# Second feed-forward products by Strassen's seven-product scheme, in a kernel of eight transformer stages

## The chip, the cores and the metric

The kernel runs on one core of one Trainium2 chip. The metric is the device time of one execution in microseconds (us). The kernel before takes 2401.51 us (median of 3 runs, 2397.78 to 2402.21).

## The reference, cut to what matters

Two blocks of two layers each run over 512 tokens of width 1024 in float32. The second block has a feed-forward part in each of its layers, and the change touches these two alone:

```python
def squared_relu_mlp(u, w1, w2):
    return jnp.square(jax.nn.relu(u @ w1)) @ w2
...
        u = squared_relu_mlp(rms_norm(h, g_ff_pre[l]), w_ff1[l], w_ff2[l])
        h = h + rms_norm(u, g_ff_post[l])
```

`w1` is 1024 x 4096 and `w2` is 4096 x 1024. Their two products have the same number of multiplications.

## The kernel before

The program is a row of eight stages (`STAGES`); `ff0` and `ff1` are the fifth and the last. All weights lie in one array `ws`, in the order in which they are used: tiles of 128 x 2048 numbers (1 MB) that hold 1024 x 256 or 512 x 512 weights.

**Three passes for float32.** Each operand is split into a rounded high part and the rest. ScalarE (ACT) copies it to the rounded type, VectorE (DVE) subtracts that copy from the original. `mm3` then issues three matmuls for each product: high x high, low x high, high x low. For weights the split makes `whi` and `wlo` (L257, L258, two halves of 128 x 1024 each); for the activations in the feed-forward, `yh` and `yl` (L355, L356). `weights` splits one tile ahead of the one in use and has the transfer of the tile after that under way: `raw` has three buffers, `whi` and `wlo` two of 128 x 2048 each.

**The feed-forward stage (`ff`).** It goes over the 4096 features in four groups of 1024. In a group, eight units (`unit`) of 24 matmuls make 128 features each for all 512 tokens, in a PSUM bank `pj` (three of them). ACT takes the relu (L1222), DVE squares it (L1223), and the result `r` is split. The second product then takes four PSUM banks, one for each 128 tokens, for each half of the 1024 output columns: 2 x 4 x 24 = 192 matmuls for a group, all of 128 x 512. DVE adds each bank into `acc` (L1247). GpSimd (POOL) does nothing in these groups. At the last group, `second_half` interleaves the norm and the transposes of the next stage (`boundary`, `norm_T`).

**The start of the stage.** Before the stage opens, `begin` has done the first 256 tokens of the first four units; when it opens, only 24 short matmuls of each of the four are left.

**What sets the order.** A scheduler turns the program into one fixed queue for each engine. An instruction waits at the head of its queue for the others by semaphores, and everything behind it waits too. SyncE (SP) issues the weight transfers in order, each when its buffer has been read.

Of the kernel before, what the change touches and what calls it, by code (L numbers as in the profile page):

```python
# [41 lines left out]
def stream_order(stages):  # L42
# [14 lines left out]
    for st in stages:  # L57
# [24 lines left out]
        elif st in ("x0", "x1"):  # L82
            for h in range(4):
                span("xq" + st[1], 256 * h)
            outw("xo" + st[1])
        elif st in ("ff0", "ff1"):
            for q in range(4):
                for j in range(4):
                    span("ff1_" + st[2], q * 1024 + j * 256)
                outw("ff2_" + st[2], q * 1024)  # L90
# [15 lines left out]
def host_arrays(inputs, stages):  # L106
# [15 lines left out]
    for n, (key, kind, sel) in enumerate(order):  # L122
        a = w[key]
        if kind == "cols":
            b = a[:, list(sel)].reshape(8, P, 256)
        else:
# [63 lines left out]

class Prog:
    def __init__(self, ctx, tc, a, out, stages):
# [4 lines left out]
        self.wt = {}  # L197

# [40 lines left out]
    def _dma(self, n):  # L239
        if n >= len(self.order) or ("r", n) in self.wt:  # L240
            return
        r = []
        for half in range(2):
            t = self.wp.tile([P, 1024], F32, tag="raw", name="raw", bufs=3)
            self.nc.sync.dma_start(out=t, in_=self.a["ws"][n, :, half * 1024:(half + 1) * 1024])
            r.append(t)
        self.wt["r", n] = r

    def _split(self, n):
        if n >= len(self.order) or n in self.wt:  # L250
            return
        self._dma(n)
        hi = self.wp.tile([P, 2048], F32R, tag="whi", name="whi", bufs=2)
        lo = self.wp.tile([P, 2048], F32R, tag="wlo", name="wlo", bufs=2)
        for half, t in enumerate(self.wt.pop(("r", n))):
            s = slice(half * 1024, (half + 1) * 1024)
            self.nc.scalar.activation(out=hi[:, s], in_=t, func=AF.Copy)  # L257
            self.nc.vector.tensor_sub(out=lo[:, s], in0=t, in1=hi[:, s].bitcast(F32))  # L258
        self.wt[n] = (hi, lo)
        self.wt["r", n] = None  # L260

    def weights(self, key):
# [6 lines left out]
        self._split(n)  # L269
        self._split(n + 1)  # L270
        self._dma(n + 2)
        hi, lo = self.wt.pop(n)
        c = 256 if self.order[n][1] == "cols" else 512
        return n, hi.rearrange("p (k c) -> p k c", c=c), lo.rearrange("p (k c) -> p k c", c=c)

    def mm3(self, ps, pairs, first=True, last=True, between=None):

        n = len(pairs)
        for k, ((ah, al), (bh, bl)) in enumerate(pairs):
            if between and k == n // 2:  # L280
# [930 lines left out]
    def ff(self, l, stage):  # L1211
        nc = self.nc
        with self.pool(f"ff{l}") as p:
            acc = [p.tile([P, D], F32, tag=f"acc{t}", name=f"acc{t}") for t in range(NT)]
            for q in range(4):
                y = []
                for j in range(4):
                    w = self.weights(f"ff1_{l}")
                    for m in range(2):
                        ps = self.unit(w, m)  # L1220
                        r = p.tile([P, S], F32, tag="r", name="r", bufs=2)
                        nc.scalar.activation(out=r, in_=ps, func=AF.Relu)  # L1222
                        nc.vector.scalar_tensor_tensor(out=r, in0=ps, scalar=0.0, in1=r, op0=ALU.max, op1=ALU.mult)  # L1223
                        y.append(self.split_y(r))
                if q == 3:
                    self.begin_out(stage, p)
                for c in range(2):
                    cs = slice(c * 512, (c + 1) * 512)
                    if q == 3 and c == 1:
                        def done(t, ps):  # L1230
                            nc.vector.tensor_tensor(out=acc[t][:, cs], in0=acc[t][:, cs], in1=ps, op=ALU.add)
                            self.boundary(t, (acc[t][:, :512], acc[t][:, 512:]), self.h[:, t, :], stage, p)

                        self.second_half(f"ff2_{l}", y, done)
                        continue
                    pa = [self.ps(tag) for tag in ("sc", "sc", "pv", "pj")]
                    for kh in range(2):
                        _, hi, lo = self.weights(f"ff2_{l}")
                        for t in range(NT):
                            tok = slice(t * P, (t + 1) * P)  # L1240
                            self.mm3(pa[t], [((y[kh * 4 + k][0][:, tok], y[kh * 4 + k][1][:, tok]), (hi[:, k, :], lo[:, k, :]))
                                             for k in range(4)], first=kh == 0, last=kh == 1)
                    for t in range(NT):
                        if q == 0:
                            self.copy(acc[t][:, cs], pa[t])
                        else:
# [219 lines left out]
```

## Time and profile before

| | us |
|---|---|
| median of 3 runs | 2401.51 |
| profiled execution | 2402.01 |
| its span, first to last instruction | 2400.2 |
| TensorE (PE) busy | 2349.0, 98% |
| DVE busy | 1278.6, 53% |
| ACT busy | 930.4, 39% |
| POOL busy | 269.9, 11% |
| stage `ff0`, about | 1346 to 1700 |
| stage `ff1`, about | 2050 to 2400 |

TensorE is busy almost without a break. Matmuls are pipelined: one is listed with the time from its start to its end, but the next starts earlier. What a matmul costs is therefore read from the distance between starts. What another engine's work costs is read from who waits for it.

### The profile page before, as it was taken

The numbers are of one execution on the slowest core, as the hardware profiler recorded it, in microseconds if no ns is written. First come the engines' busy times: TensorE is split into PE (matmuls) and PEld (weight loads), VectorE is DVE, ScalarE is ACT, GpSimd is POOL, SyncE is SP. The second block draws the span as 40 slices with busy tenths as digits, with TensorE's granted clock in tenths as the row PEclk, the third lists the DMA queues.
The fourth block names the chain that finished last, engine by engine and source line by source line (L and its number), as shares of the span: only waits on it lengthen the run. The fifth ranks groups of instructions, "written<-read, shape, count | busy, mean of one in ns | idle before, by whom it ended". The sixth has DMA issues, their size and how long they took to land.

```text
span 2400.2 us, 33303 instructions
## 1 busy us (share of the span) xinstructions
PE 2349.0 (98%) x13008; PEld 1947.0 (81%) x13008; DVE 1278.6 (53%) x2370; ACT 930.4 (39%) x1843; POOL 269.9 (11%) x315
## 2 busy tenths in 40 slices
PE   7999999999999999999999999999999999999998
PEld 7879788787888878877988888888866988888887
DVE  5364655546665546664644633435786645533434
ACT  3333333333444444453533422323465534432322
POOL 3010111101211112000200100000211201000000
PEclk9999999999999999999999999999999999999999
DMA  5433333334232322223331332322322422332322
GB/s 167 129 102 119 98 116 91 108 93 129 99 100 86 98 91 93 76 70 114 123 123 71 106 101 92 104 90 88 99 84 97 141 89 80 106 105 89 103 90 79
DMA packets 94172, 242.39 MB, mean 101 GB/s; under 512 B 26700, under 2 KB 30828, under 8 KB 94016
## 3 DMA queue, kind: packets, MB, share of 16 engines
q1 hardware_dynamic: 93216, 238.34, 30.4%
q8 instruction: 102, 1.67, 0.3%
q0 software_dynamic: 800, 1.94, 0.3%
q14 instruction: 54, 0.44, 0.1%
HBM read 215.98 MB, written 4.33 MB: 92 GB/s over the span
## 4 chain that ended last, share of the span: by engine, by line
PE 63%; DVE 4%; issue 2%; ACT 2%; POOL 2%; DMA 1%; SPq 0%; POOLq 0%; DVEq 0%; ACTq 0%
PE pj L282 14%; PE pj L284 13%; PE pj L283 13%; PE sc L282 3%; PE sc L283 3%; PE sc L284 3%; PE pv L282 2%; PE pv L284 2%; PE pv L283 2%; PE sc L1325 1%; DVE h L431 1%; PE sc L775 1%; DVE wlo L258 1%; PE pv L797 1%; PE pt L401 1%
## 5 line engine op out<-in xcount | busy, mean ns | idle before, releaser
L258 DVE TENSOR_TENSOR wlo<-raw,whi 128x1024 fp32r<-128x1024 f32 x372 | 473.4, 1294 | 498.0 <-ACT whi L257 498.0
L257 ACT ACTIVATE whi<-raw 128x1024 fp32r<-128x1024 f32 x372 | 382.7, 1055 | 538.7 <-PE pj L284 216.7
L282 PE MATMUL pj<-uh,whi 128*128 128x512 f32 (+1 forms) x1424 | 561.4, 394 | 0.8 <-ACT ho L1101 0.8
L284 PE MATMUL pj<-uh,wlo 128*128 128x512 f32 (+1 forms) x1424 | 551.8, 388 | 1.6 <-DVE wlo L258 1.6
L283 PE MATMUL pj<-ul,whi 128*128 128x512 f32 (+1 forms) x1424 | 550.6, 387 | 0.0
L282 PEld LDWEIGHTS pj<-uh,whi 128*128 128x128 f32 x1424 | 267.6, 188 | 73.7 <-issue 17.1
L284 PEld LDWEIGHTS pj<-uh,wlo 128*128 128x128 f32 x1424 | 267.6, 188 | 60.0 <-issue 3.8
L283 PEld LDWEIGHTS pj<-ul,whi 128*128 128x128 f32 x1424 | 267.9, 188 | 52.1 <-issue 2.4
L513 POOL TENSOR_TENSOR ro<-rt 128x512 f32<-128x512 f32 x74 | 112.8, 1535 | 657.6 <-DVE rt L511 587.9
L282 PE MATMUL pj<-whi,uh 128*128 128x256 f32 x608 | 174.9, 288 | 0.0
L283 PE MATMUL pj<-wlo,uh 128*128 128x256 f32 x608 | 172.5, 284 | 0.0
L284 PE MATMUL pj<-whi,ul 128*128 128x256 f32 x608 | 171.9, 283 | 0.0
L282 PE MATMUL pj<-whi,yh 128*128 128x512 f32 x416 | 164.1, 395 | 1.4 <-ACT yh L355 1.1
L283 PE MATMUL pj<-wlo,yh 128*128 128x512 f32 x416 | 162.6, 391 | 0.9 <-DVE wlo L258 0.9
L284 PE MATMUL pj<-whi,yl 128*128 128x512 f32 x416 | 162.6, 391 | 0.0
L376 POOL TENSOR_SCALAR rs<-ss 128x1 f32<-128x1 f32 x32 | 23.1, 722 | 1089.0 <-ACT bq L422 1088.8
L282 PE MATMUL sc<-whi,yh 128*128 128x512 f32 x320 | 126.8, 396 | 0.1
L283 PE MATMUL sc<-wlo,yh 128*128 128x512 f32 x320 | 125.8, 393 | 0.0
L284 PE MATMUL sc<-whi,yl 128*128 128x512 f32 x320 | 125.2, 393 | 0.0
L282 PEld LDWEIGHTS pj<-whi,uh 128*128 128x128 f32 x608 | 116.4, 191 | 4.6 <-ACT at L231 2.3
L283 PEld LDWEIGHTS pj<-wlo,uh 128*128 128x128 f32 x608 | 116.5, 192 | 0.5 <-issue 0.2
L284 PEld LDWEIGHTS pj<-whi,ul 128*128 128x128 f32 x608 | 116.4, 192 | 0.2 <-issue 0.2
(364 smaller groups left out, 3833.4 us busy)
## 6 DMA issues: line engine op xcount, KB each, us to landing
raw<-in_ws_dram SPq DMA_DIRECT2D x372, 512.0 KB, 4.0
qk<-ro SPq DMA_DIRECT2D x256, 64.0 KB, 2.0
gpre<-in_gains_dram SPq DMA_DIRECT2D x8, 512.0 KB, 5.6
gpost<-in_gains_dram SPq DMA_DIRECT2D x8, 512.0 KB, 5.2
xt<-in_x_dram SPq DMA_DIRECT2D x4, 512.0 KB, 8.1
dv<-v SPq DMA_DIRECT2D x4, 512.0 KB, 4.1
v<-dv SPq DMA_DIRECT2D x16, 128.0 KB, 4.7
h<-in_x_dram SPq DMA_DIRECT2D x4, 512.0 KB, 5.6
```

The costliest lines, as they stand in the source:

```text
L257: self.nc.scalar.activation(out=hi[:, s], in_=t, func=AF.Copy)
L258: self.nc.vector.tensor_sub(out=lo[:, s], in0=t, in1=hi[:, s].bitcast(F32))
L282: self.nc.tensor.matmul(ps, lhsT=ah, rhs=bh, start=first and k == 0, stop=False)
L283: self.nc.tensor.matmul(ps, lhsT=ah, rhs=bl, start=False, stop=False)
L284: self.nc.tensor.matmul(ps, lhsT=al, rhs=bh, start=False, stop=last and k == n - 1)
L376: nc.gpsimd.tensor_scalar(out=r[:, 0:1], in0=ss[:, 0:1], scalar1=ss[:, 1:2], scalar2=EPS, op0=ALU.add, op1=ALU.add)
L401: nc.tensor.transpose(pt[:, k * P:(k + 1) * P], b[:, (4 * g + k) * P:(4 * g + k + 1) * P], self.ident)
L431: nc.vector.scalar_tensor_tensor(out=h, in0=b, scalar=r, in1=h, op0=ALU.mult, op1=ALU.add)
L513: nc.gpsimd.tensor_tensor(out=o, in0=t[0], in1=t[1], op=op)
L775: nc.tensor.matmul(ps[:, :n], lhsT=q[hs, 0, i * P:n], rhs=q[hs, 1, :n], start=True, stop=True)
L797: nc.tensor.matmul(o[:, i * P:(i + 1) * P], lhsT=at[:, j * P:(j + 1) * P], rhs=v[h // 2][:, j, (h % 2) * P:(h % 2 + 1) * P], start=j == 0, ...
L1325: nc.tensor.matmul(ps[e][:, hp * 256 + lo:(hp + 1) * 256], lhsT=q[hs, hp, i * P:(i + 1) * P], rhs=kd[hs, g, (i - 1) * P + lo:(i + 1) * P], ...
```

## The change

**The scheme.** In seven of eight blocks of 512 features, the second product is no longer done as one sum. The left matrix (512 tokens x 512 features) is cut in halves both ways, into A11, A12 (first 256 tokens) and A21, A22; the weights (512 features x 1024 columns) into B11, B12, B21, B22 of 256 x 512. In place of eight products of quarters there are seven: A11 B11, A12 B21, S2 T2, S1 T1, S3 T3, S4 B22 and A22 T4, where each S is a sum or difference of A quarters and each T one of B quarters. A product is 12 matmuls of 128 x 512, so a block has 84 where the old way needs 96. The eighth block of each stage is done the old way, so that the norm can be interleaved with it.

**Sums on GpSimd.** `quad_sums` makes T3, T1, T2, T4 in place in the buffers that hold the weights (tag `quad`, five buffers), four instructions of 128 x 1024 for a block. `operands` makes S1 to S4 for each of the two pairs of feature chunks, j = 0, 1 of a block: four instructions of 128 x 256 each, two in tile `s12`, two in tile `s34`. Before, GpSimd had none of these.

**Splits.** Weights are split by halves of 128 x 1024 (`whi` and `wlo` now have four such buffers): 11 for a block of 512 features, four of `w1` and seven of the B's and T's, where the old way needs four and four. The left operands are split from `r`, `s12` and `s34`: 128 x 512, 256, 512 and 512 columns for each j, where two of 128 x 512 were needed.

**Banks.** A12 B21, S1 T1 and S4 B22 gather in six PSUM banks over all seven blocks (`sums`) and are added to `acc` once. The other four products go through two `pj` banks (`chain`), added to `acc` after each; the same two banks serve the units of the next block, since the third holds a sum.

The descriptor memory of the GpSimd queue shrinks too (`dynamic_dma_scratch_size=4096`). The bytes of weights stay the same.

```diff
+            for q in range(8):
+                for j in range(2):
+                    span("ff1_" + st[2], q * 512 + j * 256)
+                if q < 7:
+                    for m in range(2):
+                        out.append(("ff2_" + st[2], "quad", (q * 512 + m * P, m)))
...
+QUADS = ("B11", "B21", "T2", "T1", "T3", "B22", "T4")
...
+            for m, name in enumerate(("B11", "B12", "B21", "B22")):
+                q[name] = self.qp.tile([P, 1024], F32, tag="quad", name="quad", bufs=5)
+                self.nc.sync.dma_start(out=q[name], in_=self.a["ws"][n + m // 2, :, (m % 2) * 1024:(m % 2 + 1) * 1024])
...
+    def _fill(self, m):
+
+        while len(self.ready) < m and self.done < len(self.halves):
+            n, name = self.halves[self.done]
+            self._dma(n)
+            if n not in self.wt:
+                return
+            t = self.wt[n].get(name)
+            hi = self.wp.tile([P, 1024], F32R, tag="whi", name="whi", bufs=4)
+            lo = self.wp.tile([P, 1024], F32R, tag="wlo", name="wlo", bufs=4)
+            self.parts((hi, lo), t)
...
+    def quad_sums(self, n, first):
+
+        q = self.wt[n]
+        sub = lambda name, x, y: (self.nc.gpsimd.tensor_tensor(out=q[name], in0=q[x], in1=q[y], op=ALU.subtract))
+        if first:
+            q["T3"] = self.qp.tile([P, 1024], F32, tag="quad", name="quad", bufs=5)
+            sub("T3", "B22", "B12")
+            q["T1"] = q["B12"]
+            sub("T1", "B12", "B11")
+        else:
+            q["T2"], q["T4"] = q["B11"], q["B21"]
+            sub("T2", "B22", "T1")
+            sub("T4", "B21", "T2")
...
+            def operands(ya, yb):
+
+                h = slice(0, 256), slice(256, S)
+                s12, s34 = (p.tile([P, S], F32, tag=n, name=n, bufs=2) for n in ("s12", "s34"))
+                for out, x, z, op in ((s12[:, h[0]], ya[:, h[1]], yb[:, h[1]], ALU.add), (s12[:, h[1]], s12[:, h[0]], ya[:, h[0]], ALU.subtract),
+                                      (s34[:, h[0]], ya[:, h[0]], ya[:, h[1]], ALU.subtract), (s34[:, h[1]], yb[:, h[0]], s12[:, h[1]], ALU.subtract)):
+                    nc.gpsimd.tensor_tensor(out=out, in0=x, in1=z, op=op)
+                res = {}
+                for names, t in ((("A12", "A22"), yb), (("A11",), ya), (("S1", "S2"), s12), (("S3", "S4"), s34)):
...
+            for q in range(7):
+                ops = []
+                n = self.order.index((f"ff2_{l}", "quad", (q * 512, 0)))
+                for j in range(2):
+                    w = self.weights(f"ff1_{l}")
+                    self._dma(n)
+                    if j == 1:
+                        self._fill(2)
+                    self.quad_sums(n, j == 0)
+                    ops.append(operands(*features(w)))
+                self.pos += 2
+                chain = [self.ps("pj") for _ in range(2)]
+                for left, acc_of in (("A11", (0, 0)), ("A12", None), ("S2", (0, 1)), ("S1", None), ("S3", (1, 1)), ("S4", None), ("A22", (1, 0))):
+                    (hi, lo), = self._take(1)
...
+                        ps = chain[t] if acc_of else sums[left][t]
+                        self.mm3(ps, [([z[:, tok] for z in ops[j][left]], (hi[:, j, :], lo[:, j, :])) for j in range(2)],
+                                 first=left == "A11" if acc_of else q == 0, skip_group_check=True)
+                        if acc_of:
+                            add(2 * acc_of[0] + t, acc_of[1], ps, q == 0)
```

**Where the instructions stand.** Three places, first as it was and then as it is. In the names, the number behind a tile tells buffers apart.

POOL, start of `ff0`. Before, the last norm of the boundary is followed at once by that of the next boundary:

```order
L390 TENSOR_TENSOR bu_12019<-h_5610,gpre_11673 128x320
L378 TENSOR_SCALAR rs_12025<-ss1_12021 128x1
L379 TENSOR_TENSOR rs_12025<-rs_12025,mhalf_80 128x1
L376 TENSOR_SCALAR rs_14273<-ss_14268 128x1
L379 TENSOR_TENSOR rs_14273<-rs_14273,mhalf_80 128x1
```

Now the twelve sums of the first block stand between them (the first nine are shown). In order they are: first half of `s34` for j = 0, T3, T1, T2, first half of `s12`, T4, second halves of `s12` and `s34`, then j = 1.

```order
L439 TENSOR_TENSOR rs_12099<-rs_12099,mhalf_80 128x1
L1303 TENSOR_TENSOR s34_12434<-r_12403 128x256
L325 TENSOR_TENSOR quad_12376<-quad_12374,quad_12370 128x1024
L325 TENSOR_TENSOR quad_12370<-quad_12370,quad_12368 128x1024
L325 TENSOR_TENSOR quad_12368<-quad_12374,quad_12370 128x1024
L1303 TENSOR_TENSOR s12_12433<-r_12403,r_12430 128x256
L325 TENSOR_TENSOR quad_12372<-quad_12372,quad_12368 128x1024
L1303 TENSOR_TENSOR s12_12433<-s12_12433,r_12403 128x256
L1303 TENSOR_TENSOR s34_12434<-r_12430,s12_12433 128x256
L1303 TENSOR_TENSOR s34_12520<-r_12489 128x256
```

So `s12` of j = 0 is complete only after all four T's.

PE, a middle block, where the second product begins. Before, the first matmuls take features that were split long ago:

```order
L284 MATMUL pj_12970<-uh_11675,wlo_12855 128x512
L282 MATMUL sc_13002<-whi_12928,yh_12744 128x512
L283 MATMUL sc_13002<-wlo_12929,yh_12744 128x512
L284 MATMUL sc_13002<-whi_12928,yl_12745 128x512
L282 MATMUL sc_13002<-whi_12928,yh_12776 128x512
```

Now 16 matmuls that need only j = 0 come first (`yh_13077`, `yh_13073`, `yh_13081`); the last of them, and the first of j = 1 (`yh_13161`, then `yh_13165`), are:

```order
L342 MATMUL sc_12602<-whi_13197,yh_13081 128x512
L342 MATMUL pj_13178<-whi_13089,yh_13077 128x512
L343 MATMUL pj_13178<-wlo_13090,yh_13077 128x512
L344 MATMUL pj_13178<-whi_13089,yl_13078 128x512
L342 MATMUL pt_12565<-whi_13093,yh_13161 128x512
L342 MATMUL pj_13177<-whi_13089,yh_13165 128x512
```

The last unit's output is thus wanted 16 matmuls after that unit ends.

DVE, where the second product of a middle block ends. Before, the four adds follow two splits, and nothing stands between them:

```order
L258 TENSOR_TENSOR wlo_13065<-raw_13012,whi_13064 128x1024
L258 TENSOR_TENSOR wlo_13065<-raw_13014,whi_13064 128x1024
L1247 TENSOR_TENSOR acc0_12182<-acc0_12182,sc_13002 128x512
L1247 TENSOR_TENSOR acc1_12183<-acc1_12183,sc_13003 128x512
L1247 TENSOR_TENSOR acc2_12184<-acc2_12184,pv_13004 128x512
L1247 TENSOR_TENSOR acc3_12185<-acc3_12185,pj_13005 128x512
```

Now (B21's buffer `quad_13004` holds T4, and the `raw` rows are weights of the next block's units):

```order
L416 TENSOR_TENSOR wlo_13248<-quad_13004,whi_13247 128x1024
L416 TENSOR_TENSOR wlo_13270<-raw_13251,whi_13269 128x1024
L1285 TENSOR_TENSOR acc2_12366<-acc2_12366,pj_13177 128x512
L1285 TENSOR_TENSOR acc3_12367<-acc3_12367,pj_13178 128x512
L416 TENSOR_TENSOR wlo_13286<-raw_13253,whi_13285 128x1024
L416 TENSOR_TENSOR wlo_13308<-raw_13289,whi_13307 128x1024
L1285 TENSOR_TENSOR acc2_12366<-acc2_12366,pj_13177 128x512
L1285 TENSOR_TENSOR acc3_12367<-acc3_12367,pj_13178 128x512
```

The last add out of the first `chain` bank (`pj_13177`), which the next block's first unit writes next, stands behind a split of weights for that block's third unit (`wlo_13308`).

## Rows read from the trace of the kernel before

**Rows 1.** The page: busy us (share of the span) and instructions

```profile
PE 2349.0 (98%) x13008; PEld 1947.0 (81%) x13008; DVE 1278.6 (53%) x2370; ACT 930.4 (39%) x1843; POOL 269.9 (11%) x315
```

**Rows 2.** Busy us (instructions) by stretch: PE, PEld, DVE, ACT, POOL; clock, DMA share, GB/s

```profile
1345.00:1700.00 355.00, 351.70 (x1647) 294.43 (x1646) 157.13 (x182) 117.45 (x164) 14.44 (x20) 1.00 0.28 95
2050.00:2380.00 330.00, 328.86 (x1511) 274.64 (x1510) 134.52 (x159) 103.85 (x138) 2.17 (x5) 1.00 0.27 93
```

**Rows 3.** Timeline of PE in `ff1` (start, us, instruction): two starts, 24 matmuls apart

```profile
2139.82 0.39 PE L282 MATMUL pj<-uh,whi 128*128 128x512 f32 x1
...
2145.26 0.39 PE L282 MATMUL pj<-uh,whi 128*128 128x512 f32 x1
```

**Rows 4.** From one unit's end to its split features: timelines of PE, ACT, DVE

```profile
1428.47 0.39 PE L282 MATMUL pj<-uh,whi 128*128 128x512 f32 x1
...
1428.67 0.60 ACT L1222 ACTIVATE r<-pj 128x512 f32<-128x512 f32 x1 [2.95 <-PE pj L284]
...
1429.30 0.69 DVE L1223 SCALAR_TENSOR_TENSOR r<-pj,r 128x512 f32<-128x512 f32 x1 [2.13 <-ACT r L1222]
...
1430.02 0.63 ACT L355 ACTIVATE yh<-r 128x512 fp32r<-128x512 f32 x1 [0.76 <-DVE r L1223]
...
1430.68 0.69 DVE L356 TENSOR_TENSOR yl<-r,yh 128x512 fp32r<-128x512 f32 x1 [0.70 <-ACT yh L355]
```

**Rows 5.** ACT and DVE: a weight half on ACT, two on DVE, an add

```profile
1433.93 1.06 ACT L257 ACTIVATE whi<-raw 128x1024 fp32r<-128x1024 f32 x1 [3.28 <-PE pj L283]
...
1403.05 2.36 DVE L258 TENSOR_TENSOR wlo<-raw,whi 128x1024 fp32r<-128x1024 f32 x2 [3.61 <-ACT whi L257]
...
1483.07 0.69 DVE L1247 TENSOR_TENSOR acc<-acc,sc 128x512 f32<-128x512 f32 x1 [1.39 <-PE sc L284]
```

**Rows 6.** POOL: ns min/median/max of its two kinds of wide instructions

```profile
L513 POOL TENSOR_TENSOR ro<-rt x74: 1275/1305/2287, 38.2 to 1793.0; 128x512 f32<-128x512 f32 x74
...
L390 POOL TENSOR_TENSOR bu<-h,gpre x28: 876/1523/1584, 627.6 to 2049.0; 128x320 f32<-128x320 f32 x28
```

**Rows 7.** Timelines of DVE and POOL where both are busy

```profile
103.84 0.68 DVE L511 TENSOR_TENSOR rt<-pj,sin 128x512 f32<-128x512 f32 x1
104.44 3.43 DVE L258 TENSOR_TENSOR wlo<-raw,whi 128x1024 fp32r<-128x1024 f32 x2
...
102.74 1.31 POOL L513 TENSOR_TENSOR ro<-rt 128x512 f32<-128x512 f32 x1 [45.30 <-DVE rt L511]
104.65 2.13 POOL L513 TENSOR_TENSOR ro<-rt 128x512 f32<-128x512 f32 x1 [0.60 <-DVE rt L511]
```

**Rows 8.** Start of `ff0`: PE's first short matmul and first full one; first relu, square

```profile
1346.20 0.28 PE L282 MATMUL sc<-uh,whi 128*128 128x256 f32 x1
...
1357.72 0.40 PE L282 MATMUL pj<-uh,whi 128*128 128x512 f32 x1
...
1349.28 0.60 ACT L1222 ACTIVATE r<-sc 128x512 f32<-128x512 f32 x1 [3.71 <-PE sc L284]
...
1349.91 0.69 DVE L1223 SCALAR_TENSOR_TENSOR r<-sc,r 128x512 f32<-128x512 f32 x1 [3.56 <-ACT r L1222]
```

**Rows 9.** Transfers: issue to landing of weight halves (KB, median us); SP's issue before `ff0`

```profile
raw<-in_ws_dram SPq DMA_DIRECT2D x372, 512.0 KB, 4.0
...
1339.42 0.42 SPq L368 DMA_DIRECT2D gpost<-in_gains_dram  x1
```

**Rows 10.** A long wait of PE: timeline, then the clock by stretch (columns as Rows 2)

```profile
1128.88 1.17 PE L401 MATMUL pt<-ident,bu 128*128 128x128 f32 x8 [3.99 <-DVE bu L393]
...
1131.13 0.63 PE L282 MATMUL sc<-whi,yh 128*128 128x512 f32 x1
1131.56 0.63 PE L283 MATMUL sc<-wlo,yh 128*128 128x512 f32 x1
...
1130.00:1131.00 1.00, 1.00 (x4) 0.81 (x3) 1.00 (x2) 1.00 (x3) 0.00 (x0) 0.50 0.00 0
1132.00:1133.00 1.00, 1.00 (x4) 0.81 (x3) 1.00 (x2) 0.00 (x0) 0.00 (x0) 0.50 0.97 393
```

**Rows 11.** PE's waits for weight splits (us in total, times, longest)

```profile
PE pj L284 <- DVE wlo L258: 1.6, 1, 1.6
...
PE pj L283 <- DVE wlo L258: 0.9, 1, 0.9
```

More of the change, by code (lines that the diff above doesn't have):

```diff
@@ L86, in stream_order @@
         elif st in ("ff0", "ff1"):
[L87 to L90, printed above, removed]
+            for q in range(8):
[5 more added lines that the diff above has]
+                else:
+                    for c in range(2):
+                        out.append(("ff2_" + st[2], "rows", (q * 512, c * 512)))
         elif st == "sw":
@@ L1213, in ff @@
         with self.pool(f"ff{l}") as p:
+            self.qp = p
             acc = [p.tile([P, D], F32, tag=f"acc{t}", name=f"acc{t}") for t in range(NT)]
-            for q in range(4):
-                y = []
-                for j in range(4):
-                    w = self.weights(f"ff1_{l}")
[L1219 to L1226, printed above, removed]
-                for c in range(2):
[L1228 to L1246, printed above, removed]
-                            nc.vector.tensor_tensor(out=acc[t][:, cs], in0=acc[t][:, cs], in1=pa[t], op=ALU.add)
@@ new lines, in ff, with add, features @@
+            sums = {}
+            def add(t, c, ps, new=False):
+                out = acc[t][:, c * 512:(c + 1) * 512]
+                if new:
+                    self.copy(out, ps, "s")
+                else:
+                    nc.vector.tensor_tensor(out=out, in0=out, in1=ps, op=ALU.add)
+            def features(w):
+                y = []
+                for m in range(2):
+                    ps = self.unit(w, m)
+                    r = p.tile([P, S], F32, tag="r", name="r", bufs=4)
+                    nc.scalar.activation(out=r, in_=ps, func=AF.Relu)
+                    nc.vector.scalar_tensor_tensor(out=r, in0=ps, scalar=0.0, in1=r, op0=ALU.max, op1=ALU.mult)
+                    y.append(r)
+                return y
@@ new lines, in ff @@
+            y = []
+            for j in range(2):
+                y += [self.split_y(z) for z in features(self.weights(f"ff1_{l}"))]
+                if j == 0:
+                    for t in range(2):
+                        add(t, 0, sums["A12"][t])
+                        add(2 + t, 1, sums["S1"][t])
+                        add(t, 1, sums["S1"][t])
+                        add(t, 1, sums["S4"][t])
+            self.qp = None
+            self.begin_out(stage, p)
+            w = [self.weights(f"ff2_{l}")[1:] for _ in range(2)]
@@ new lines, in part, with done @@
+            def part(ps, t, c):
+                tok = slice(t * P, (t + 1) * P)
+                self.mm3(ps, [((y[k][0][:, tok], y[k][1][:, tok]), (w[c][0][:, k, :], w[c][1][:, k, :])) for k in range(4)])
+                add(t, c, ps)
+            def done(t):
+                self.boundary(t, (acc[t][:, :512], acc[t][:, 512:]), self.h[:, t, :], stage, p)
+            for t in range(2 if self.next else NT):
+                for c in range(2):
+                    part(self.ps("pj"), t, c)
+                done(t)
```

91 lines of the change are left out of this document (63 added, 28 removed).

## The prediction

> **What bounds the kernel now.** I read the busy shares first: TensorE (PE) is busy 98% of the span [rows 1], and in the two feed-forward stages more than that, 351.7 of 355 us and 328.9 of 330 us [rows 2]. So these stages are priced by matmuls, as long as PE never waits. A matmul of 128 x 512 costs the distance between starts: 24 of them take 2145.26 - 2139.82 = 5.44 us, 0.2267 us each [rows 3]. VectorE (DVE) works under half of that time there, GpSimd (POOL) 2 to 14 us of it [rows 2]. The question is whether the removed matmuls stay removed, or come back as waits.
>
> **What the change removes.** Twelve matmuls in each of seven blocks in two stages: 168 x 0.2267 = 38.1 us. All of it is on the path, since PE has no slack there.
>
> **What it adds beside PE.** A block of 512 features is now 4 units x 24 + 84 = 180 matmuls, 40.8 us. The work of the others in a block, from rows:
> - DVE: 11 weight halves at 1.14 (two in 2.36 with their overlap [rows 5]), 12.5; squares 4 x 0.6 and adds 8 x 0.6 (0.69 alone [rows 4, 5], some 0.6 in a row), 7.2; left operands 2 x (0.6 + 0.35 + 0.6 + 0.6), 4.3. Together 24 us.
> - POOL: an instruction of 512 columns takes 1.29, one of 320 columns 0.88 [rows 6], so 2.16 ns a column on 0.19 us. That gives 2.4 for 1024 columns and 0.74 for 256, as estimates; the trace has neither. A block's 4 T sums and 8 S sums are 9.6 + 5.9 = 15.5 us.
>
> By shares both fit into 40.8 us. But the two engines do not run side by side. A DVE pair of weight splits alone takes 2.36 us [rows 5]; where a POOL instruction falls into it the pair takes 3.43 and the POOL instruction 2.13 in place of 1.3 [rows 7]. 1.07 more on the one and 0.83 on the other is what comes out if each runs alone and they take turns. A DVE instruction that reads PSUM (L511) beside a POOL instruction keeps its 0.68 [rows 7]. So splits from SBUF (`wlo`, `yl`) exclude POOL's sums; squares and adds, which read PSUM, do not. The Trainium skill ("SBUF — State Buffer", section "Who interferes with whom") speaks against this change in the same way: the shared port pair is an exclusive lock, and a DVE instruction with two SBUF inputs blocks GpSimd for its whole length or is blocked by it. The trace agrees (3.43 against 2.36), and the sum without that lock is the first rival below. The skill also has a price for the sums ("GPSIMD Engine Reference", section "Elementwise — side-by-side cycle accounting"): 4497 ns for 2048 columns of float32, so about 2.25 for 1024, an estimate. By it each T sum would be 0.15 us shorter and the total some 2 us lower.
>
> With that I follow the fixed queues, alternating whenever both want to go. From a unit's end to its square's end takes 1.5 us, to `yh` 2.2, to `yl` 2.9 [rows 4].
>
> **First block of a stage (q = 0).** Only four half units of 2.88 us are left when the stage opens: 11.52 us [rows 8], and then the products begin. POOL's first sum waits for the first square, 4.4 us in [rows 8]; the T's behind it wait too, though their weights are there (the transfers can go at about 1339, where SP issued its last ones before the stage [rows 9], and land in some 4 to 8 us). Complete `s12` for j = 0 needs 0.74 + 3 x 2.4 + 0.74 + 2.4 + 0.74 = 11.8 us of POOL, and between these DVE takes its turns with B11, B21, two left operands and T2: 3 x 1.15 + 0.95 = 4.4 us. So it is there at 4.5 + 11.8 + 4.4 = 20.7, and its `yh` at 21.4. PE has 12 matmuls to do until then, to 14.2: **7.2 us of waiting**. Next, ACT's queue has the relu of the last unit behind the `yh` of `s34`: 21.5 + 0.65 + 0.6, its square 0.7, T1's copy beside it, its `yh` 0.65: 24.4, where PE had two matmuls, to 21.9: **2.5**. Then the two `yl` of that unit, which alternate with T1's split and the sums of j = 1, at 26.8 and 27.9: **1.9**. Sum 11.6 us. PE then has been idle for over 3 us twice. After a wait of 3.99 us the granted clock was 0.50, the lower level, for some 3 us, and matmuls came 0.43 apart in place of 0.23 [rows 10]; seven of them cost 1.5 us. I add that once: 13.1 us a stage, 26 in both. Bounds: 5.3 a stage if nothing excludes anything (POOL's 11.8 us alone still end at 16.3, 2.8 late, and the relu costs 2.5), 16 if the clock falls twice and POOL is 10% slower.
>
> **Begin of the products, blocks 1 to 6.** Count from the products' first matmul. Sixteen matmuls that need only j = 0 cover 3.6 us, and the last unit's `yh` is there at 2.2: no wait. The wait comes at matmul 28, at 6.35 us, which rewrites the first `chain` bank and needs the add out of it. That add stands on DVE behind all four left operands of j = 1, and these need POOL. By turns: square 1.5, first half of `s12` 2.34, `yl` 2.95, second half of `s12` 3.7, `yl` 4.05, `s34` 4.8, `yl` of `s12` 5.45, of `s34` 6.15, add 6.75: 0.5 late with the semaphore. And the square is late itself: POOL can form T2 only after B11's split, and T2 and T4 (31.1 to 35.95 after the previous block's products began) stand ahead of `s12` and `s34` of j = 0. By turns their `yl` end at 40.55, the third unit's square at 41.15, POOL's next sum at 42.0, the splits of T2 and T1 at 44.3, while the products begin at 42.8; the last unit's square follows at 44.3 in place of 43.6, 0.65 late. **1.2 us a block**, 12 blocks, 14 us. Bounds 0 and 2.4 (another POOL turn).
>
> **End of the products, blocks 0 to 5.** Behind the seven products stands the next block's first unit, which needs the last add out of the first `chain` bank. On DVE that add is behind a weight split for the third unit (`wlo_13308`), and this split can start at 17.9 (its buffer is read out at matmul 72, at 16.8; ACT's copy 1.06). SP sends B21 and B22 of the next block when T4's split is done, at 12.0; two issues of 0.42 and 4.0 to land [rows 9] make 16.5 to 17.1. Then T3's sum starts at once and keeps the lock to about 19.3; the split ends at 20.5, the add at 21.1. PE wants the bank at 19.5: **1.5 us a block**, 12 blocks, 18 us. Bounds: 0.2 if the transfer lands after 17.9, 2.6 if just before it. Before, nothing stood between the last matmul and the four adds, and no unit wrote the bank that an add was reading.
>
> **What costs nothing.** The eight closing adds of the six sums (4.8 us of DVE) lie under a unit of 10.9 us; the tail keeps its 24 matmuls a token block; the bytes of weights are the same. Splits by halves in the other stages could at best give back the waits for `wlo` of the whole kernel, 2.5 us [rows 11]; I take 0, within 2 either way.
>
> **Sum.** 26 + 14 + 18 - 38 = +20 us on the profiled execution's 2402.0 (span 2400.2 and 1.8 around it): 2422. The median of the runs is 0.5 lower, so 2422 stands within the rounding: 0.9% slower.
>
> **Rivals.**
> 1. The sums hide: no exclusion, or POOL so quick that it doesn't matter. The first blocks cost 2 x 5.3, the ends 12 x 0.2, the begins 0: 13 - 38 = -25, about 2377. For it: by busy shares everything fits (24 and 15.5 of 40.8 us), and the 16 matmuls ahead of j = 1 cover the last unit. Against it: [rows 7].
> 2. The middle blocks hide, the first blocks don't: if the transfer lands late enough and POOL is a little ahead, 26 + 2 - 38 = -10, 2392. Faster, too.
> 3. Only one of the two ends of a block waits: 26 + 16 - 38 = +4, 2406, which is even.
> 4. Slower still: DVE and POOL together become the bound. Their 24 and 15.5 us, if nearly all of it excludes, are 39.7 of 40.8 us. A turn more at each end of a block (2.4 and 2.6 us x 12) makes 60 + 32 - 38 = +54, 2456. It decides once a T sum is held back past the next unit's end.
> 5. The change does not do what it says. The queue of PE shows 84 matmuls a block, so hardly.
>
> **How the numbers follow.** A change of 0.2% (4.8 us) is about the least that a measurement tells here. Forecast (2407 to 2436): 0.47. Rival 4 (2436 to 2460): 0.15. Rival 3 (2397 to 2407): 0.11. Rival 2 (2386 to 2397): 0.13. Rival 1 (2372 to 2386): 0.13. Rival 5: 0.01. So slower 0.62, same 0.11, faster 0.27. For 8 in 10 the range leaves out the lower half of rival 1 and the upper part of rival 4: 2380 to 2446; the forecast's own range is 2407 to 2436.
>
> **What would show it.** PE's matmuls 168 fewer, at the same distance. POOL 2 x 7 x 15.5 = 217 us busier or more, its T sums near 2.4 us alone and 3.5 where they meet a split. In the first block of each stage a wait of PE for ACT's `yh` of `s12` of several us, with the clock at the lower level behind it. In each later block two waits of 1 to 2 us, one of `pj` for the `acc` add at the seventh product's end, one at the third product's begin. I am wrong if PE stays as busy in these stages as it was, or if its waits are for transfers or for `whi` instead.

## The result, and the profile after

The changed kernel takes 2424.9 us (median of 4 runs, 2424.0 to 2428.5) beside 2400.7 for the kernel before (4 runs, 2397.8 to 2402.2): 1.0105 times as long, 95% interval 1.0088 to 1.0123. The profiled execution took 2428.45 us with a span of 2426.7, 26.5 us more than the span before. So 168 matmuls left the program and it became 1% slower.

First the page's busy shares, then the two feed-forward stages as windows (columns as in [rows 2]; the second stage begins about 9 us later than before, and its window is 20 us later, so that it leaves out the stage's first 8 us; it is still 330 us long). In the windows read PE against the length of the stretch: 331.9 of 353 us, 307.8 of 330, where before it was 351.7 of 355 and 328.9 of 330 [rows 2]. The matmuls went, and PE now stands still for some 6% of each stage, and its mean granted clock there is 0.98. VectorE went up from 157 to 244 us in the first stage, GpSimd from 14 to 131.

```profile
PE 2340.2 (96%) x12840; PEld 1919.5 (79%) x12840; DVE 1486.8 (61%) x2540; ACT 1019.5 (42%) x1949; POOL 521.3 (21%) x483
```

```profile
1342.00:1695.00 353.00, 331.90 (x1467) 267.60 (x1468) 243.89 (x248) 146.52 (x198) 130.76 (x94) 0.98 0.26 91
2070.00:2400.00 330.00, 307.80 (x1319) 246.30 (x1318) 229.23 (x227) 135.59 (x178) 122.53 (x83) 0.98 0.25 85
```

What PE waited for in the whole run (us in total, times, longest one). The first row is the add out of a `chain` bank: 22 waits, twelve near the begin of a block's products and ten at the end. The others did not stand in the profile before in this size ([rows 11] had 0.9 and 1.6 for `wlo`).

```profile
PE pj L342 <- DVE acc L1285: 23.7, 22, 2.1
...
PE pj L344 <- DVE yl L416: 6.0, 14, 1.3
PE sc L342 <- ACT whi L415: 5.0, 2, 2.9
PE sc L343 <- DVE wlo L416: 4.3, 12, 0.4
PE pj L342 <- ACT yh L415: 4.0, 2, 2.0
```

**A middle block.** Timelines of PE, POOL and DVE in the second block of the first stage (start, us, engine, line; in brackets the idle time before and what ended it). The products start at 1407.74 and the next block's first unit at 1430.70: 22.96 us for 84 matmuls, which at the pitch of [rows 3] take 19.04. Three short waits stand at the begin (0.36, 0.26, 0.47), one of 1.69 at the end.

```profile
1407.74 0.39 PE L342 MATMUL pj<-whi,yh 128*128 128x512 f32 x1
...
1410.53 0.50 PE L343 MATMUL sc<-wlo,yh 128*128 128x512 f32 x1 [0.36 <-DVE wlo L416]
...
1413.40 0.50 PE L344 MATMUL pj<-whi,yl 128*128 128x512 f32 x1 [0.26 <-DVE yl L416]
...
1415.98 0.50 PE L342 MATMUL pj<-whi,yh 128*128 128x512 f32 x1 [0.47 <-DVE acc L1285]
...
1430.70 0.47 PE L342 MATMUL pj<-uh,whi 128*128 128x512 f32 x1 [1.69 <-DVE acc L1285]
```

```profile
1422.85 6.02 POOL L325 TENSOR_TENSOR quad<-quad 128x1024 f32<-128x1024 f32 x2 [8.90 <-DMA quad<-in_ws_dram]
```

```profile
1424.71 1.91 DVE L416 TENSOR_TENSOR wlo<-raw,whi 128x1024 fp32r<-128x1024 f32 x1 [0.25 <-ACT whi L415]
1427.42 2.53 DVE L416 TENSOR_TENSOR wlo<-raw,whi 128x1024 fp32r<-128x1024 f32 x1 [0.81 <-ACT whi L415]
1429.88 1.27 DVE L1285 TENSOR_TENSOR acc<-acc,pj 128x512 f32<-128x512 f32 x2
```

Read the last four rows together: two T sums start when the next block's weights land, 15.1 us after the products began. A split that takes 1.2 alone (two in 2.36 in [rows 5]) takes 1.91 beside the first and 2.53 beside the second, and the adds that PE needs stand right behind that second split.

**A first block.** Rows of PE, then a window of 10 us, then POOL, DVE and ACT in the first block of the first stage. With the wait ahead of them its 84 matmuls take 29.9 us in the place of 19.0 (29.3 in the second stage). PE waits 2.00, 1.34 and 2.17 us; from 1359 to 1372 the granted clock is at its lower level (0.50 in the window, 17 matmuls in 10 us).

```profile
1358.04 0.50 PE L342 MATMUL pj<-whi,yh 128*128 128x512 f32 x1 [2.00 <-ACT yh L415]
...
1360.11 0.80 PE L344 MATMUL pj<-whi,yl 128*128 128x512 f32 x1 [1.34 <-DVE yl L416]
...
1366.92 1.22 PE L342 MATMUL sc<-whi,yh 128*128 128x512 f32 x2 [2.17 <-ACT whi L415]
...
1372.24 0.53 PE L343 MATMUL pt<-wlo,yh 128*128 128x512 f32 x1
```

```profile
1360.00:1370.00 10.00, 7.72 (x17) 5.49 (x18) 8.59 (x9) 3.65 (x7) 8.56 (x6) 0.50 0.22 73
```

```profile
1349.59 9.05 POOL L325 TENSOR_TENSOR quad<-quad 128x1024 f32<-128x1024 f32 x3
...
1359.74 2.54 POOL L325 TENSOR_TENSOR quad<-quad 128x1024 f32<-128x1024 f32 x1
1362.25 1.71 POOL L1303 TENSOR_TENSOR s<-s,r 128x256 f32<-128x256 f32 x1
...
1349.86 6.57 DVE L416 TENSOR_TENSOR wlo<-quad,whi 128x1024 fp32r<-128x1024 f32 x2 [1.04 <-ACT whi L415]
...
1357.06 0.94 ACT L415 ACTIVATE yh<-r 128x512 fp32r<-128x512 f32 x2 [5.31 <-DVE r L1293]
...
1363.99 0.63 ACT L415 ACTIVATE yh<-s 128x512 fp32r<-128x512 f32 x1 [4.26 <-POOL s L1303]
```

Two splits that take 2.36 as a pair in [rows 5] take 6.57 beside three T sums that take 9.05. The second square stands behind them on DVE, and ACT's `yh` waits 5.31 us for it.

### The profile page after: what moved, and what is told of

Read it like the earlier page. It is cut to its first block, busy times and chain, and to the rows that moved or that the text cites. A ratio compares the mean times of both kernels' runs of the same rounds, so it can differ in the third digit from the quotient of the medians.

```text
span 2426.7 us, 33679 instructions
## 1 busy us (share of the span) xinstructions
PE 2340.2 (96%) x12840; PEld 1919.5 (79%) x12840; DVE 1486.8 (61%) x2540; ACT 1019.5 (42%) x1949; POOL 521.3 (21%) x483
## 4 chain that ended last, share of the span: by engine, by line
PE 51%; DVE 7%; POOL 7%; issue 4%; ACT 3%; DMA 1%; POOLq 0%; DVEq 0%; SPq 0%; ACTq 0%
PE pj L342 13%; PE pj L343 12%; PE pj L344 12%; POOL s L1303 3%; DVE wlo L416 3%; POOL quad L325 2%; ACT whi L415 2%; PE sc L343 2%; PE sc L344 2%; PE sc L342 2%; PE pv L342 1%; PE sc L1448 1%; DVE h L491 1%; PE sc L835 1%; PE pv L343 1%
## 5 line engine op out<-in xcount | busy, mean ns | idle before, releaser
L416 DVE TENSOR_TENSOR wlo<-raw,whi 128x1024 fp32r<-128x1024 f32 x316 | 413.1, 1310 | 316.7 <-ACT whi L415 303.2
L342 PE MATMUL pj<-uh,whi 128*128 128x512 f32 (+1 forms) x1424 | 565.4, 397 | 18.3 <-DVE acc L1285 18.1
L342 PEld LDWEIGHTS pj<-uh,whi 128*128 128x128 f32 x1424 | 269.0, 189 | 97.8 <-issue 21.8
L342 PE MATMUL pj<-whi,yh 128*128 128x512 f32 x556 | 221.7, 399 | 10.3 <-DVE acc L1285 5.7
L344 PE MATMUL pj<-whi,yl 128*128 128x512 f32 x556 | 219.6, 397 | 6.0 <-DVE yl L416 6.0
L343 PE MATMUL pj<-wlo,yh 128*128 128x512 f32 x556 | 218.2, 393 | 0.0
L325 POOL TENSOR_TENSOR quad<-quad 128x1024 f32<-128x1024 f32 x56 | 149.8, 2676 | 159.8 <-DMA quad<-in_ws_dram 100.9
L416 DVE TENSOR_TENSOR wlo<-quad,whi 128x1024 fp32r<-128x1024 f32 x98 | 147.3, 1515 | 55.1 <-ACT whi L415 52.1
L342 PE MATMUL pj<-whi,uh 128*128 128x256 f32 x608 | 174.7, 287 | 0.0
L342 PEld LDWEIGHTS pj<-whi,yh 128*128 128x128 f32 x556 | 105.2, 189 | 40.6 <-DVE acc L1285 10.8
L415 ACT ACTIVATE whi<-quad 128x1024 fp32r<-128x1024 f32 x98 | 103.3, 1057 | 77.9 <-PE pj L343 45.4
L344 PEld LDWEIGHTS pj<-whi,yl 128*128 128x128 f32 x556 | 105.0, 189 | 34.9 <-DVE yl L416 12.4
L343 PEld LDWEIGHTS pj<-wlo,yh 128*128 128x128 f32 x556 | 105.4, 190 | 20.1 <-issue 0.5
```

The lines of the kernel that those rows point to most:

```text
L325: sub = lambda name, x, y: (self.nc.gpsimd.tensor_tensor(out=q[name], in0=q[x], in1=q[y], op=ALU.subtract))
L415: self.nc.scalar.activation(out=dst[0], in_=src, func=AF.Copy)
L416: self.nc.vector.tensor_sub(out=dst[1], in0=src, in1=dst[0].bitcast(F32))
```

## Experiments

Nine kernels, each made from the changed one. The rows of the first table are medians; the second column is the time of the kernel before on the same chip; "products" is the time from a block's first product to the next unit, in a middle block of the first stage, against 19.04 without a wait; "first block" is the same for the stage's first block, with the wait just ahead of its first product.

| kernel | us | before | products | first block |
|---|---|---|---|---|
| changed kernel | 2424.9 | 2400.7 | 22.96 | 29.9 |
| e1: no sums | 2369.7 | 2401.9 | 19.95 | 19.4 |
| e2: sums that nobody reads | 2414.1 | 2401.9 | 22.3 | 28.0 |
| e3: no T sums | 2390.7 | 2401.9 | 21.2 | 23.1 |
| e4: no S sums | 2402.1 | 2401.9 | 21.5 | 26.3 |
| e5: all sums on VectorE | 2373.4 | 2401.5 | 19.40 | 25.7 |
| e6: S on VectorE, T on GpSimd | 2412.0 | 2401.5 | 21.7 | 26.7 |
| e7: T sums later | 2445.2 | 2401.5 | 21.86 | 30.3 |
| e8: T on VectorE, S on GpSimd | 2388.1 | 2402.9 | 20.69 | 25.0 |
| e9: e5, B22 done third | 2381.8 | 2402.9 | 20.3 | 24.1 |

**e1 to e4: what of the loss is the sums, and what in them.** The question was whether the lost time comes from PE waiting for the sums' results, or from GpSimd holding VectorE up. TensorE's queue is the same in all four as in the changed kernel, and so is VectorE's but for two pairs of left-operand splits that change places in the first block of each stage. e1 takes the sums out:

```diff
-            sub("T3", "B22", "B12")
-            sub("T1", "B12", "B11")
...
-                    nc.gpsimd.tensor_tensor(out=out, in0=x, in1=z, op=op)
+                s12, s34 = ya, yb
```

> Leaves out every sum on GpSimd (T's and S's are replaced by the unsummed weights and features, so the products are of other numbers); matmuls, splits, adds and the order on VectorE stay. Theory A (the sums make the waits, by their length and by excluding the splits): of some 69 us that TensorE loses in the two stages about 60 go, 2365 us. Rival B (the longer VectorE and ScalarE queues, three more weight splits and 1.75 times the left operands a block, make them): at most 10 us go, 2415 or more.

Measured: 2369.7 us (2367.4 to 2372.3), ratio 0.9866 [0.9851, 0.9881]. The page and the longest wait for an add (line numbers are 5 lower here): PE's share is 98% again, and the 23.7 us of the changed kernel are 3.8.

```profile
PE 2319.5 (98%) x12840; PEld 1911.0 (81%) x12840; DVE 1398.5 (59%) x2540; ACT 1017.7 (43%) x1949; POOL 271.6 (11%) x315
```

```profile
PE pj L337 <- DVE acc L1280: 3.8, 10, 0.4
```

So the scheme with its 84 matmuls, 11 splits and moved adds is worth 32 us, close to the 38 that the matmuls are worth. All the rest, 55 us, comes with the sums. e2 keeps the sums as they are, but writes them into buffers that nobody reads:

```diff
-            sub("T3", "B22", "B12")
+            q["X"] = self.qp.tile([P, 1024], F32, tag="quad", name="quad", bufs=5)
+            sub("B22", "B12")
...
+                s12, s34 = ya, yb
```

> GpSimd does sums of the same number, length and place in its queue, but into buffers that nobody reads; the products use the unsummed numbers as in e1_no_sums. Theory A1 (excluding the splits is most of it in the middle blocks): the waits at the end of a block stay (some 1.7 us each), half of those at the begin, a third of the first blocks': about 2396 us. Theory A2 (only the time to wait for a sum counts): as e1_no_sums, 2365.

Measured: 2414.1 us (2412.4 to 2415.7), ratio 1.005 [1.0035, 1.0065]. The wait for the adds is nearly all there, and VectorE is busy for 1477.7 us, 79 more than in e1, for the same instructions:

```profile
PE pj L343 <- DVE acc L1286: 20.4, 22, 2.6
```

Of the 55 us, 44 come without anyone waiting for a sum. That VectorE is held up while GpSimd adds is the main cause, and it weighs more than I had expected of it; waiting for results is the other 11. (Sums that nobody reads still read the weights, and may free a buffer later; among PE's waits in e2 there is none for a transfer.) e3 and e4 take out one kind of sums each, by the lines of e1's diff that make T, and those that make S.

> Leaves out the four sums of weights of each block (T's are unsummed weights), keeps the S sums. Theory A: the waits at the ends go (12 x 1.6), most of the first blocks' (2 x 8) and half of the begins' (12 x 0.7): about 2381 us. Rival B: 2415 or more.

> Leaves out the sums of features (S's are unsummed features), keeps the T sums. Theory A: the waits at the begins go (12 x 1.5) and half of the first blocks' (2 x 6), those at the ends stay: about 2395 us. Rival B: 2415 or more.

Measured: 2390.7 us (ratio 0.9952 [0.9936, 0.9969]) without the T's, 2402.1 (1.0 [0.9991, 1.001]) without the S's. Above e1 that is 21 us for the S sums alone and 32 for the T sums alone, 53 of the 55 together: the two kinds add up, and neither is free. Both cost more than expected (2381 and 2395). The T's make the end wait (without them the waits for adds are 9.3 us in total, 0.5 at most; without the S's 19.5 us).

**e5, e6, e8: the same sums on the other engine.** If GpSimd's sums hold VectorE for as long as they run, VectorE should lose little by doing them itself. e5 is the full computation, with two words changed:

```diff
-        sub = lambda name, x, y: (self.nc.gpsimd.tensor_tensor(out=q[name], in0=q[x], in1=q[y], op=ALU.subtract))
+        sub = lambda name, x, y: (self.nc.vector.tensor_tensor(out=q[name], in0=q[x], in1=q[y], op=ALU.subtract))
...
-                    nc.gpsimd.tensor_tensor(out=out, in0=x, in1=z, op=op)
+                    nc.vector.tensor_tensor(out=out, in0=x, in1=z, op=op)
```

> The full computation, with all sums on VectorE (seven 0.6 to 1.2 us instructions more in its queue for each pair, some 7.4 us a block), none on GpSimd. Theory A (the price is GpSimd's length and its turns against the splits): the middle blocks lose about 1 us each and the first blocks about 4: 2380 to 2388 us, faster than the kernel before. Rival B (VectorE's own load is what PE waits for, so more of it makes more waits): 2410 or more.

Measured: 2373.4 us (2372.6 to 2374.7), ratio 0.9885 [0.987, 0.99]: 51.5 us less than the changed kernel, and 28 less than the kernel before. It is below the range expected (2380 to 2388), and the fastest of the kernels that do the full computation. Its page and the waits for adds; then the groups of its T sums and of the splits of `r` that are 512 columns wide; then, on PE, the first product of a middle block and the first matmul of the next unit:

```profile
PE 2322.0 (98%) x12840; PEld 1914.2 (81%) x12840; DVE 1497.4 (63%) x2708; ACT 1018.8 (43%) x1949; POOL 271.2 (11%) x315
```

```profile
PE pj L342 <- DVE acc L1285: 0.8, 2, 0.4
```

```profile
L325 DVE TENSOR_TENSOR quad<-quad 128x1024 f32<-128x1024 f32 x56 | 68.2, 1218 | 1.0 <-DMA quad<-in_ws_dram 0.5
...
L416 DVE TENSOR_TENSOR yl<-r,yh 128x512 fp32r<-128x512 f32 x36 | 24.7, 685 | 5.6 <-ACT yh L415 5.6
```

```profile
1402.49 0.39 PE L342 MATMUL pj<-whi,yh 128*128 128x512 f32 x1
...
1421.89 0.39 PE L342 MATMUL pj<-uh,whi 128*128 128x512 f32 x1
```

The same two groups in the changed kernel, in the same columns (busy us, mean ns, idle before):

```profile
L325 POOL TENSOR_TENSOR quad<-quad 128x1024 f32<-128x1024 f32 x56 | 149.8, 2676 | 159.8 <-DMA quad<-in_ws_dram 100.9 <-DVE wlo L416 43.1 <-issue 14.6
...
L416 DVE TENSOR_TENSOR yl<-r,yh 128x512 fp32r<-128x512 f32 x36 | 40.6, 1129 | 23.8 <-ACT yh L415 23.8
```

Compare DVE's busy time in the three pages. Without sums it is 1398.5 us; with the sums on GpSimd 1486.8, for the same 2540 instructions; with the sums on DVE itself 1497.4. Giving 168 sums away took 10.6 us off DVE. The other 88 came back as splits that last longer, such as these `yl`, 685 ns against 1129, while a T sum in DVE's own queue is done in 1.2 us.

The 51.5 us may not be the engine's alone. With the T sums on DVE, in e5 and in e8, the scheduler also gives DVE another order at the end of a block (in e5 a few of PE's matmuls at the begin change places, too): the add out of the first `chain` bank now stands ahead of the split behind which it stood (in the changed kernel two splits, then the adds at 1429.88). Rows of DVE in e5:

```profile
1419.69 1.22 DVE L325 TENSOR_TENSOR quad<-quad 128x1024 f32<-128x1024 f32 x1
1420.83 0.68 DVE L1285 TENSOR_TENSOR acc<-acc,pj 128x512 f32<-128x512 f32 x1
1421.42 1.22 DVE L416 TENSOR_TENSOR wlo<-raw,whi 128x1024 fp32r<-128x1024 f32 x1
```

The end waits, some 20 us of the changed kernel's time, may be gone for this reason too; e1, with the old order and no sums at all, keeps one of 0.38 in ten blocks. The old place of the sums with the new order of the adds was not run. What GpSimd's sums cost in a given order is shown by e1 and e2.

e6 moves only the S sums to VectorE, e8 only the T sums (one of the two lines of e5's diff each).

> The full computation, with the S sums on VectorE and the T sums on GpSimd. Theory A: the begin's dependence on GpSimd goes, and T's of the first block no longer wait for the first square; the ends' waits (T sums against the splits) stay: 2398 to 2408 us, near the kernel without S sums. Rival B: 2425 or more.

> The full computation; the T sums of 1024 columns run on VectorE, the S sums of 256 columns stay on GpSimd. It is the fourth corner beside after (both on GpSimd), e6_s_dve and e5_all_dve. Exclusion theory: every GpSimd sum takes its turn with VectorE's splits, the short ones too, and the S sums stand ahead of the left operands; e3_no_t, which keeps only the S sums on GpSimd, was 21 us above e1_no_sums, and moving all sums to VectorE cost 4, so 2390 to 2398. Rival, only a long T sum holds a split back for long enough to be late: near e5_all_dve, 2373 to 2380, with first blocks near 25 us and products of the middle blocks under 20 us.

Measured: e6 2412.0 us (2407.6 to 2414.9), ratio 1.0049 [1.0032, 1.0066], a little above what I had expected; e8 2388.1 (2387.6 to 2388.1), ratio 0.994 [0.9923, 0.9956], 2 us below the exclusion theory's range and 8 us above the rival's. With e5 as the corner where nothing is on GpSimd, the S sums there cost 14.7 us, the T sums 38.6, and both 51.5, nearly the sum of the two. The order of the adds changes with the T sums alone (e6 keeps the old one), so it is the T's 38.6 that hold its part. In e8 the wait for adds is small (twelve of them, 5.6 us in total, 0.5 at most), and the rest of a block's 1.3 us above e5 is other short waits at its begin.

**e7: is it the moment at which the T sums start?** T3 and T1 start when their weights land, shortly before the products end. e7 puts them behind the square of the next block's first unit, by one sum of a single column that needs it:

```diff
+            self.nc.gpsimd.tensor_tensor(out=q["T3"][:, 0:1], in0=y[:, 0:1], in1=y[:, 1:2], op=ALU.subtract)
             sub("T3", "B22", "B12")
...
-                    self.quad_sums(n, j == 0)
-                    ops.append(operands(*features(w)))
+                    if j == 1:
+                        self.quad_sums(n, False)
+                    yy = features(w)
+                    if j == 0:
+                        self.quad_sums(n, True, yy[0])
+                    ops.append(operands(*yy))
```

> The kernel as changed, but with a one-column GpSimd instruction ahead of T3 that reads the first unit's square, so that T3 and T1 run after that unit and not beside the splits at the end of the seven products; VectorE's queue is the same. Theory A: the waits at the ends (12 times about 1.3 us above what is left without sums) go, the later T2 and T4 push the sums of j = 0 and 1 back and the begins grow by up to 1 us: 2410 to 2422. If the waits at the ends come from VectorE's queue alone: 2425, ends unchanged.

Measured: 2445.2 us (2443.9 to 2447.7), ratio 1.0185 [1.017, 1.02]. The expectation missed, though the end wait did go (0.38 left, products 21.86 in place of 22.96). Rows of PE, POOL and DVE (L417 is the split, L1294 the square):

```profile
1458.66 0.50 PE L343 MATMUL pj<-whi,yh 128*128 128x512 f32 x1 [2.40 <-DVE r L1294]
...
1442.23 11.89 POOL L325 TENSOR_TENSOR quad<-quad 128x1024 f32<-128x1024 f32 x4
1454.08 0.92 POOL L1304 TENSOR_TENSOR s<-r 128x256 f32<-128x256 f32 x1
...
1446.29 2.76 DVE L417 TENSOR_TENSOR wlo<-quad,whi 128x1024 fp32r<-128x1024 f32 x1 [0.58 <-ACT whi L416]
...
1450.35 4.05 DVE L417 TENSOR_TENSOR yl<-r,yh 128x512 fp32r<-128x512 f32 x2 [0.70 <-ACT yh L416]
1456.51 1.50 DVE L417 TENSOR_TENSOR yl<-s,yh 128x512 fp32r<-128x512 f32 x2 [2.11 <-ACT yh L416]
1457.92 0.68 DVE L1294 SCALAR_TENSOR_TENSOR r<-pj,r 128x512 f32<-128x512 f32 x1
```

Now all four T sums run in one row of 11.9 us. Beside them a split lasts 2.76 us and two `yl` 4.05; and the S sums that complete `s12` and `s34` for j = 0 stand behind them and start only at 1454.08, so that DVE waits 2.11 us for their `yh`. The last square stands behind that on DVE, and PE waits 2.4 us for it in every block. So part of the loss here is a wait for results, not for a split that is held. In both places that were tried the T sums make PE wait; only which wait it is changes.

**e9: the first block of e5.** What remains in e5 is the first block, 25.7 and 24.3 us for 84 matmuls; its longest wait was for ACT's copy of T2. e9 does S4 B22 third in place of sixth, so that more matmuls need no T sum:

```diff
-QUADS = ("B11", "B21", "T2", "T1", "T3", "B22", "T4")
+QUADS = ("B11", "B21", "B22", "T2", "T1", "T3", "T4")
```

> e5_all_dve (all sums on VectorE) with one change: of the seven products of a block, S4 B22 is done third in place of sixth, so that 36 matmuls need no T sum, where before 24 did. In e5_all_dve the first block of a stage takes 25.7 and 24.3 us for 84 matmuls that need 19.0, and its longest wait is of PE for ACT's copy of T2 (2.7 us). If that chain of T sums is what the first block waits for, the wait goes and the first blocks come down to 20 to 22.5 us: 2364 to 2370. Rival, the left operands' own chain of squares, sums and splits is what comes last: the wait changes its name and stays, 2371 to 2376.

Measured: 2381.8 us (2380.6 to 2385.2), ratio 0.9916 [0.9901, 0.9931], 8 more than e5. Both theories missed. The first blocks gained 1.6 and 1.8 us, and the wait there did change its name (now two waits of 1.3 and 1.2 for the squares). But the middle blocks lost 0.2 to 1.1 us each, 8.7 in total. Rows of DVE and PE near the end of such a block's products:

```profile
1415.39 2.49 DVE L325 TENSOR_TENSOR quad<-quad 128x1024 f32<-128x1024 f32 x2 [0.51 <-DMA quad<-in_ws_dram]
1417.79 1.28 DVE L1285 TENSOR_TENSOR acc<-acc,pj 128x512 f32<-128x512 f32 x2
...
1418.62 0.47 PE L342 MATMUL pj<-whi,yh 128*128 128x512 f32 x1 [0.71 <-DVE acc L1285]
```

S4 B22, which goes to banks of its own, had stood between the last two products that share the `chain` banks. Moved away, it no longer covers the adds between them: the last product now wants a bank whose adds stand on DVE behind the next block's first two T sums, and PE waits for them in every middle block.

## Why the prediction was right, step by step

The time came out 3 us from the forecast and by the mechanism that it named. That it came so close is luck in part: the begins were 10 us short, the first blocks 5 too long, and 6 us came back in stages that were put at nothing. The sum was made for the profiled execution, which became 26.4 us longer and not 20.

- **Removal, -38.1.** It holds: PE has 168 matmuls fewer, and full units still take 21.76 us for 96, the pitch of [rows 3]. e1, with the sums gone, shows 32 of it.
- **Durations of the sums.** Undisturbed, a T sum takes 2.40 us (it was 2.4 as an estimate from [rows 6]) and an S sum 0.74 (0.74). The Trainium skill's figure ("GPSIMD Engine Reference", section "Elementwise — side-by-side cycle accounting": 4497 ns for 2048 columns), halved to 2.25 as an estimate, is 0.15 below what the trace shows. With their waits for the lock the four groups of sums are busy for 250 us, where 217 was the undisturbed sum.
- **Exclusion.** It holds: the rows of the middle block show it, and e2 beside e1 shows its price. By the Trainium skill ("SBUF — State Buffer", section "Who interferes with whom") a DVE instruction with two SBUF inputs contends with a GpSimd instruction that reads SBUF, and the port pair that they share is an exclusive lock; the trace agrees, with a split of 2.53 in place of 1.2. Rival 1 (no exclusion, 2377) fell; e5 comes out near its time by having no sums on GpSimd.
- **First blocks, 26 forecast, 21.1 measured** (10.9 and 10.2). The place was right, the make-up not. I had 11.6 us of waits, first of all 7.2 for the `yh` of `s12`. That `yh` came at 1364.6, 20.3 us after the stage's first short matmul on `sc` (21.4 in the text). But PE was already late by then: the splits of B11 and B21, held by three T sums, kept the second square back, and PE waited 2.00 and 1.34 for the `yh` and the `yl` of plain A11, which I had taken as covered. So the waits sum to only 5.5 us, some 6 from start to start. The clock made up for it: I had counted seven matmuls at the lower level, 1.5 us, from one wait of 4 us [rows 10] (and "over 3 us twice" does not follow from the 7.2, 2.5 and 1.9 of the text); here, with three waits of 1.3 to 2.2 in a row, 22 matmuls from 1360.11 to 1372.24 went at 0.43 to 0.5, some 4.8 us. In the second stage the waits were 2.00, 1.33 and 2.86; the clock rose again between the last two (granted 0.50 in 2079.5 to 2082, 1.00 in 2083 to 2085, 0.50 in 2086 to 2089), and the matmuls at the lower level cost 3.2 us.
- **Begins, 1.2 forecast, 2.05 measured** (the sixth middle block, which has no end wait, takes 21.10 and 21.07). The bank's wait came as named: 0.47 against 0.5. In place of one late square of 0.65 there were two short waits, for the `wlo` of T1 (0.36) and a `yl` (0.26). The waits sum to 1.1, but a wait is listed from the modelled end of the matmul before it. From start to start the three cost 1.6 (0.75, 0.65 and 0.86 in the place of 0.23 each), and the matmul behind each starts 0.1 late, so that nearly all of the 2.05 stands at these three places.
- **Ends, 1.5 in twelve blocks forecast, some 1.9 in ten measured.** Block 0 of a stage has no end wait: its banks are not added by DVE but copied into `acc` by ACT, so no split stands ahead. In the others the bank, the add and the split ahead of it were those of the text, but the sum that held the split was another: the transfer landed at 15.1 us and not at 16.5 to 17.1, so T3 was done in time, and T1, right behind it, held the lock. In two blocks of the second stage (end waits of 1.97 and 1.84) the next block's units took 1.7 us longer, which I had not counted: the rows below show one of them, a wait of 1.97 at the end and the clock at 0.84 and 0.73 around and behind it.

```profile
2149.68 0.47 PE L342 MATMUL pj<-uh,whi 128*128 128x512 f32 x1 [1.97 <-DVE acc L1285]
```

```profile
2148.00:2152.00 4.00, 2.32 (x8) 1.89 (x9) 3.27 (x4) 0.81 (x1) 0.00 (x0) 0.84 0.46 160
2152.00:2156.00 4.00, 4.00 (x15) 3.22 (x14) 0.00 (x0) 0.00 (x0) 0.00 (x0) 0.73 0.40 137
```

- **Sum of the two stages, +20 forecast, about +32 measured**: 21 for the first blocks, 44 for twelve middle ones (3.9 to 4.4 each, 2.05 for the last of a stage), 3.4 for slower units, -38. Some 2 us of the stages are not in these terms.
- **Other stages, 0 forecast, -6 measured.** Starts of PE's matching matmuls, from the trace of before (L282) and after (L342): the same point of the program comes at 1346.20 in [rows 8] and at 1344.36 here, at 1726.95 and 1740.09 (behind the first feed-forward stage), at 2053.32 and 2062.24 (ahead of the second). So the lag goes from -1.8 to +13.1, back to +8.9, and ends at +26.5. Between the stages PE's waits fell from 7.6 to 3.7 us; the waits for `wlo` and `yh` there (0.9 and 1.1) are gone. Splitting weights by halves may be the reason, which no run here isolates. Without these 6 us the kernel would have come out near 2431.

```profile
1726.95 0.40 PE L282 MATMUL pj<-uh,whi 128*128 128x512 f32 x1
...
2053.32 0.36 PE L282 MATMUL pv<-uh,whi 128*128 128x256 f32 x1
```

```profile
1344.36 0.28 PE L342 MATMUL sc<-uh,whi 128*128 128x256 f32 x1
...
1740.09 0.40 PE L342 MATMUL pj<-uh,whi 128*128 128x512 f32 x1
...
2062.24 0.36 PE L342 MATMUL pv<-uh,whi 128*128 128x256 f32 x1
```

- **Rivals.** Rivals 2 and 3 fell with the middle blocks, where both ends wait; rival 5 with the count of matmuls. Rival 4 (2456) did not come true either, but it was not far: e7, which only moves the T sums, takes 2445.

## What to carry to other kernels

Work that is moved to an engine with a low busy share is not free when that engine and a busy one shut each other out: look first for a stretch of the trace where both work at once, and compare the pair's durations with those alone. Here the busier engine did a T sum in half the time, and the kernel that left all sums there was 51 us faster, part of it perhaps by the order of its adds. A saving in the bound engine's work pays only if the adds that free its banks and the operands that open its next phase do not stand behind a held instruction in another queue.

## What the runs showed of the hardware

- GpSimd's sums lengthen VectorE's splits by about as much as VectorE would need to do the sums: 88 us more on it for the same instructions, against 99 more with the sums in its own queue. For the expectation of e2 I had put the exclusion alone at some 30 us of the kernel's time; it was 44.
- The granted clock stayed at the lower level (1.2 GHz, 0.50) from 1359 to 1372 in the first block of the first stage, where PE waited 2.00, 1.34 and 2.17 us with a few matmuls between; after a single wait of 3.99 us it took some 3 us to recover [rows 10]. In the second stage's first block, with waits of 2.00, 1.33 and 2.86, it fell twice, for 3 to 4 us each. Of the four end waits of 1.8 to 2.2 us, those of 1.97 and 1.84 were followed by some 3 us at the lower level; one of 2.15 and another of 1.97 were not.
- A T sum costs 2.40 us on GpSimd and 1.22 on VectorE.
